# The last expert of a mixture-of-experts layer: where the other rows are normed and stored, and in what precision its down-projection runs

## The chip, the cores and the metric

The kernel runs on one core of a Trainium2 chip. The metric is the device time of one execution in microseconds (us), and the figure that counts is the median over runs. The engines are TensorE (PE, with its weight loads as PEld), VectorE (DVE), ScalarE (ACT), GpSimd (POOL) and SyncE (SP). Each runs its own instructions in order and waits for the others by semaphores. Transfers are issued from an engine's queue and carried out by 16 DMA engines that all queues share.

## The reference, cut to what matters

One layer works on 1024 latent tokens of 1024 features (float32). After a token mixer, the tokens `h` go through an expert-choice mixture of experts: each of 16 experts takes the 128 tokens with the highest affinity to it, and what the experts return is summed by token, normed, scaled and added to `h`.

```python
def ec_moe(x_tok, w_router, w_gate, w_up, w_down):
    t = x_tok.shape[1]
    cap = CAP_FACTOR * t // N_EXPERTS
...
    g, idx = lax.top_k(jnp.swapaxes(aff, 1, 2), cap)
    xs = jax.vmap(lambda xt, ix: xt[ix])(x_tok, idx)
    hg = jnp.einsum('becd,edf->becf', xs, w_gate)
    hu = jnp.einsum('becd,edf->becf', xs, w_up)
    y = jnp.einsum('becf,efd->becd', jax.nn.silu(hg) * hu, w_down) * g[..., None].astype(xs.dtype)
    return jax.vmap(lambda ix, val: jnp.zeros((t, D_MODEL), val.dtype)
                    .at[ix.reshape(-1)].add(val.reshape(-1, D_MODEL)))(idx, y)
...
        ff = ec_moe(xn, w_router[layer], w_gate[layer], w_up[layer], w_down[layer])
        h = h + g2 * rmsnorm(ff, norm_post_ffn[layer])
```

A token may be taken by several experts or by none, and its norm needs the sum over all of them. So no row that the last expert takes can be normed before that expert is done; the other rows can.

## The kernel before, in words

The part in question begins at line 1492 and fills the second half of the span. The 16 experts run one after the other. An expert's weights come as 24 tiles of 512 KB (six chunks of four: gate, up, gate, up, and two of the down-projection). `load_raw` (line 841) loads them on SP's queue into pages of two pools, 23 (`pgA`) and 7 (`pgX`), as early as pages come free; SP's order is the program's (`manual_schedule`). On the other engines the order is made by a scheduler at build time, from the program's order and its own estimates of durations.

`chunk` (line 1455) splits each tile on ScalarE and VectorE (`split`, line 161) into a high part `whi` and a rest `wlo`, both float32r. `mm3` (line 165) then makes one float32 product out of three float32r matmuls. The tokens `xh_`, `xl_` are split in the same way. `prod` (line 1467) makes `hg` and `hu`, 24 matmuls each for one half of the hidden features; `glu` (line 1486) makes `act` = silu(hg) * hu; `tsplit` (line 1448) transposes `act` on TensorE and splits it into `ach`, `acl`. The down-projection (line 1521) multiplies these by the last two chunks into two banks `pys`. For experts 0 to 14, `y` = `pys` times the gate value `g` is added to the rows `idx` of `ffS` in DRAM by an indirect scatter with accumulation, on POOL's queue (line 1534). `route(e + 1)` (line 1428) finds the next expert's rows and gathers them from `hS`, which holds `h`; `cur[2]` is the tile `xs` with the gathered rows. The output `out` has been filled with `h` long before.

The last expert's `y` does not go to DRAM. During its first `hg`, line 1509 makes `oht`, a one-hot matrix for each of the eight tiles of 128 tokens (`tt` holds the compared positions). At the end of the loop SP loads `bcG2` (the gain times the gate, broadcast) and the eight tiles of `ffS` into `fr` (line 1544). After the down-projection `y` is split into `yh`, `yl` (lines 1558 and 1559), and for each tile four matmuls with `oht` place the rows of `y` (`added`), two additions on VectorE put them onto `fr`, and a square on ScalarE sums each row (line 1582). Tiles are taken in pairs. `rsqrt` (line 215) is a chain of small VectorE steps, 13 for a pair and 10 for a single column. `final` (line 1562) scales `fr` by the root and by `bcG2` and adds it to `out` with an accumulating store on POOL's queue (line 1571).

Of the kernel before, what the change touches and what calls it, by code (L numbers as in the profile page):

```python
# [10 lines left out]
F32 = mybir.dt.float32  # L11
# [35 lines left out]
TGR = ((0, 1), (2, 3), (4, 5), (6, 7))  # L47
TD = 1
SUMB = ("ee", "eb", "bb", "ee", "be", "bb", "ee", "bb")
# [27 lines left out]
TA = (0, 2)  # L77
TP = ()
# [74 lines left out]
def build(tc, nc, I, out, dbg=None):  # L153
# [4 lines left out]
    def f(ap):  # L158
        return ap.bitcast(F32)

    def split(hi, lo, src, eng=V):
        S.activation(hi, src, AF.Copy)  # L162
        eng.tensor_sub(lo, src, f(hi))  # L163

# [6 lines left out]
    with es:  # L171
# [1282 lines left out]

        def chunk(e, c, eng=V):
            r = []
            for q in range(4):
                if not raws:
                    load_raw(pgX if (nraw[0] - NR0) % (NPA + NPX) < NPX else pgA)
                raw = raws.popleft()  # L1460
                hi = spl.tile([P, 2, 512], F32R, name="whi")
                lo = spl.tile([P, 2, 512], F32R, name="wlo")
                split(hi, lo, raw, eng)
                r.append((hi, lo))
            return r
# [20 lines left out]
        def glu(hg, hu):  # L1486
            a = x1.tile([P, 512], F32, name="act", bufs=2)
            S.activation(a, hg, AF.Silu)
            V.tensor_mul(a, a, hu)
            return a  # L1490

# [4 lines left out]
        for e in range(E):  # L1496
# [3 lines left out]
            for fh in range(2):  # L1500
                hg = eacc("hg")
                prod(hg, xh_, xl_, chunk(e, 2 * fh) if e or fh else first)
                if fh:
                    tsplit(acts[0], 0, ach, acl)
                elif e + 1 < E:
                    nxt = route(e + 1)
                else:

                    oht = page(pgA, "oht", F32R, (P, KT, P))
                    tt = sm.tile([P, KT], F32, name="tt")  # L1510
                    for t in range(KT):
                        V.tensor_scalar(tt[:, t:t + 1], cur[3][:, 0:1], -BIG - t * P, None, op0=OP.add)
                    V.tensor_tensor(out=oht, in0=late["iota"][:, None, :].to_broadcast([P, KT, P]),
                                    in1=tt[:, :, None].to_broadcast([P, KT, P]), op=OP.is_equal)
                hu = eacc("hu")
                prod(hu, xh_, xl_, chunk(e, 2 * fh + 1))
                acts.append(glu(hg, hu))
            if e + 1 < E:
                xh_, xl_ = xsplit(nxt[2], nxt[4])
            pys = [eacc("pyy") for _ in range(2)]  # L1520
            for c in range(2):
# [16 lines left out]
        fr = []  # L1538
        bc["G2"] = page(pgA, "bcG2")
        load_bc("G2")  # L1540
        for t in range(KT):

            fr.append(page(pgA, "ffr"))
            SY.dma_start(out=fr[t], in_=ffS[t * P:(t + 1) * P, :])
        yh, yl = page(pgA, "yh", F32R), page(pgA, "yl", F32R)
        fp = {}

        def sums(t):
            k = SUMB[t]
            return [bank([P, 512], "pff") if c == "b" else eacc("pff") for c in k]  # L1550

        def added(t):
            for dh, sl in enumerate(halves):
                PE.matmul(fp[t][dh], oht[:, t, :], yh[:, sl], start=True, stop=False)
                PE.matmul(fp[t][dh], oht[:, t, :], yl[:, sl], start=False, stop=True)

        for dh, sl in enumerate(halves):
            S.activation(yh[:, sl], pys[dh], AF.Copy, scale=g[:, 0:1])
            V.scalar_tensor_tensor(yl[:, sl], pys[dh], g[:, 0:1], f(yh[:, sl]), op0=OP.mult, op1=OP.subtract)
        sg, rg = [], []  # L1560

        def final(k):
            for j, t in enumerate(TGR[k]):
                r = rg[k][:, j:j + 1]
                if t in TA:
                    S.activation(fr[t], fr[t], AF.Copy, scale=r)
                elif t in TP:
                    V.tensor_scalar(fr[t], fr[t], r, None, op0=OP.mult)
                else:
                    V.scalar_tensor_tensor(fr[t], fr[t], r, bc["G2"], op0=OP.mult, op1=OP.mult)  # L1570
                G.dma_start(out=out[t * P:(t + 1) * P, :], in_=fr[t], accum_op=OP.add)

        for i, grp in enumerate(TGR):
            w = len(grp)
            ss = sm.tile([P, w], F32, name=f"ssf{w}")
            for k, t in enumerate(grp):
                junk = page(pgA, "sqf")
                fp[t] = sums(t)
                added(t)
                for dh, sl in enumerate(halves):  # L1580
                    V.tensor_add(fr[t][:, sl], fp[t][dh], fr[t][:, sl])
                S.activation(junk, fr[t], AF.Square, accum_out=ss[:, k:k + 1])
                if t in TA + TP:
                    G.tensor_mul(fr[t], fr[t], bc["G2"])
                if i and k == TD:
                    final(i - 1)
            rg.append(rsqrt(ss, D, w))
        final(len(TGR) - 1)
# [15 lines left out]
```

## Time and profile before

| | |
|---|---|
| time, median of 3 runs | 1399.57 us (1394.0 to 1402.64) |
| time of the profiled execution | 1401.37 us |
| its span | 1399.6 us |
| mean granted TensorE clock | 0.941 |
| TensorE busy | 1259.0 us (90%) |
| VectorE busy | 1104.3 us (79%) |
| ScalarE busy | 805.7 us (58%) |
| GpSimd busy | 70.8 us (5%) |
| moved to and from DRAM | 247 GB/s over the span |

Busy shares are means over stages with different limits, so they don't say what bounds a given stage. For that a stretch of the span is read by itself, in the views whose rows stand below. Matmuls are pipelined: the time from the start of one to the start of the next is what one costs. The profile was taken of one execution; its span is 1.8 us shorter than its time.

### The profile page before, as it was taken

The numbers are of one execution on the slowest core, as the hardware profiler recorded it, in microseconds if no ns is written. First come the engines' busy times: TensorE is split into PE (matmuls) and PEld (weight loads), VectorE is DVE, ScalarE is ACT, GpSimd is POOL, SyncE is SP. The second block draws the span as 40 slices with busy tenths as digits, with TensorE's granted clock in tenths as the row PEclk, the third lists the DMA queues.
The fourth block names the chain that finished last, engine by engine and source line by source line (L and its number), as shares of the span: only waits on it lengthen the run. The fifth ranks groups of instructions, "written<-read, shape, count | busy, mean of one in ns | idle before, by whom it ended". The sixth has DMA issues, their size and how long they took to land.

```text
span 1399.6 us, 18794 instructions
## 1 busy us (share of the span) xinstructions
PE 1259.0 (90%) x6457; PEld 1028.7 (73%) x6457; DVE 1104.3 (79%) x2005; ACT 805.7 (58%) x1191; POOL 70.8 (5%) x56
## 2 busy tenths in 40 slices
PE   6999998999989699789762999999999999999990
PEld 3587886887878578677652888888888888877770
DVE  6963666988778667698686799999999998888885
ACT  6632112443434444453331888888888888888762
POOL 0000000000000000000001000000000001201012
PEclk8999999999999899999775999999999999999995
DMA  9359456554486963432287899999999999999736
GB/s 351 117 109 325 133 159 208 162 164 136 142 160 182 235 218 110 136 124 95 76 311 275 278 364 389 374 376 376 379 373 378 377 379 379 354 345 350 267 120 120
DMA packets 143376, 346.67 MB, mean 248 GB/s; under 512 B 17456, under 2 KB 59952, under 8 KB 142640
## 3 DMA queue, kind: packets, MB, share of 16 engines
q1 hardware_dynamic: 115520, 310.34, 63.4%
q0 software_dynamic: 5616, 20.45, 6.1%
q10 hardware_dynamic: 22144, 14.68, 3.7%
q8 instruction: 51, 0.84, 0.2%
q14 instruction: 45, 0.37, 0.1%
HBM read 296.65 MB, written 48.77 MB: 247 GB/s over the span
## 4 chain that ended last, share of the span: by engine, by line
PE 47%; DVE 8%; ACT 2%; issue 1%; DMA 1%; SPq 0%; POOL 0%; POOLq 0%; ACTq 0%; DVEq 0%
PE hg L167 4%; PE hg L168 4%; PE hg L166 4%; PE hu L166 4%; PE hu L167 4%; PE hu L168 4%; PE pyy L167 4%; PE pyy L168 4%; PE pyy L166 4%; PE ptt L1479 2%; PE pl L921 1%; DVE nm L1099 1%; PE ptt L1451 1%; PE pf L799 1%; PE ps L1090 1%
## 5 line engine op out<-in xcount | busy, mean ns | idle before, releaser
L163 DVE TENSOR_TENSOR wlo<-raw,whi 128x1024 fp32r<-128x1024 f32 x384 | 450.1, 1221 | 30.8 <-ACT whi L162 24.5
L162 ACT ACTIVATE whi<-raw 128x1024 fp32r<-128x1024 f32 x384 | 396.1, 1066 | 61.7 <-PE hu L168 24.9
L1103 ACT ACTIVATE e<-ps,nm 128x1280 f32<-128x1280 f32 x64 | 84.4, 1325 | 68.5 <-DVE nm L1099 61.3
L1099 DVE TENSOR_REDUCE nm<-ps 128x1 f32<-128x1280 f32 x64 | 92.8, 1485 | 16.0 <-PE ps L1090 15.9
L167 PE MATMUL pyy<-wlo,ach 128*128 128x512 f32 x256 | 101.3, 396 | 3.5 <-DVE wlo L163 3.1
L166 PE MATMUL hu<-whi,xsh 128*128 128x512 f32 x256 | 101.9, 398 | 0.0
L168 PE MATMUL hg<-whi,xsl 128*128 128x512 f32 x256 | 101.2, 395 | 0.8 <-DVE xsl L163 0.8
L167 PE MATMUL hg<-wlo,xsh 128*128 128x512 f32 x256 | 101.8, 398 | 0.0
L166 PE MATMUL hg<-whi,xsh 128*128 128x512 f32 x256 | 101.3, 396 | 0.0
L167 PE MATMUL hu<-wlo,xsh 128*128 128x512 f32 x256 | 100.8, 394 | 0.0
L168 PE MATMUL pyy<-whi,acl 128*128 128x512 f32 x256 | 100.2, 391 | 0.0
L168 PE MATMUL hu<-whi,xsl 128*128 128x512 f32 x256 | 99.9, 390 | 0.0
L1135 ACT ACTIVATE ath<-ptr 128x512 fp32r<-128x512 f32 (+1 forms) x96 | 47.5, 525 | 90.7 <-PE ptr L1130 90.4
L166 PE MATMUL pyy<-whi,ach 128*128 128x512 f32 x256 | 98.9, 402 | 0.0
L1090 PE MATMUL ps<-KK,q 128*128 128x512 f32 (+1 forms) x384 | 91.0, 384 | 7.8 <-ACT e L1103 6.2
L1090 PEld LDWEIGHTS ps<-KK,q 128*128 128x128 f32 x384 | 65.1, 202 | 18.8 <-ACT e L1103 7.4
L679 PE MATMUL pf<-xh,wl 128*128 128x512 f32 x192 | 77.7, 405 | 0.0
L677 PE MATMUL pf<-xl,wh 128*128 128x512 f32 x192 | 77.3, 403 | 0.0
L675 PE MATMUL pf<-xh,wh 128*128 128x512 f32 x192 | 77.0, 401 | 0.0
L1138 DVE TENSOR_TENSOR atl<-ptr,ath 128x512 fp32r<-128x512 f32 (+1 forms) x96 | 55.6, 596 | 13.8 <-ACT ath L1135 13.6
L167 PEld LDWEIGHTS pyy<-wlo,ach 128*128 128x128 f32 x256 | 48.2, 188 | 18.0 <-DVE wlo L163 8.2
L167 PEld LDWEIGHTS hg<-wlo,xsh 128*128 128x128 f32 x256 | 48.9, 191 | 11.5 <-DVE wlo L163 1.1
(293 smaller groups left out, 2728.8 us busy)
## 6 DMA issues: line engine op xcount, KB each, us to landing
raw<-in_we SPq DMA_DIRECT2D x384, 512.0 KB, 9.5
wa<-in_wa SPq DMA_DIRECT2D x64, 256.0 KB, 4.8
wraw<-in_wF SPq DMA_DIRECT2D x20, 512.0 KB, 6.4
waw<-in_wa SPq DMA_DIRECT2D x16, 512.0 KB, 5.9
q<-qS SPq DMA_DIRECT2D x64, 128.0 KB, 4.9
mS<-hl SPq DMA_DIRECT2D x48, 128.0 KB, 4.2
vS<-hv ACTq DMA_DIRECT2D x20, 256.0 KB, 6.5
KK<-kS SPq DMA_DIRECT2D x16, 320.0 KB, 4.9
```

The source lines that it names most:

```text
L162: S.activation(hi, src, AF.Copy)
L163: eng.tensor_sub(lo, src, f(hi))
L166: PE.matmul(ps, wh, mh, start=first, stop=False)
L167: PE.matmul(ps, wh, ml, start=False, stop=False)
L168: PE.matmul(ps, wl, mh, start=False, stop=last)
L675: PE.matmul(ps, wh[:, kt, :], xh[kt][:, sl], start=first, stop=False)
L677: PE.matmul(ps, wh[:, kt, :], xl[kt][:, sl], start=False, stop=False)
L679: PE.matmul(ps, wl[:, kt, :], xh[kt][:, sl], start=False, stop=last)
L1090: PE.matmul(ps[:, m, k0:k0 + n], q[:, m, j, :], KK[:, m, k0:k0 + n], start=(j == 0), stop=(j == 1))
L1099: V.tensor_reduce(out=c[1][-1], in_=c[0][:, m, :], axis=AX.X, op=OP.max, negate=True)
L1103: S.activation(e, c[0][:, m, :], AF.Exp, bias=c[1][3 + m], accum_out=l[:, m:m + 1])
L1138: V.tensor_sub(x[1], x[2], f(x[0]))
```

## The change

- Before expert 15's first `hu`: `bcG2` is loaded (SP), the rows of `ffS` that the last expert takes are gathered into `ffg`, and the eight tiles of `ffS` are loaded into `fr`, both on POOL's queue. `oht` and `tt` are gone.
- `final(k)` now squares a pair of tiles of `fr` as they are after 15 experts, takes the root, scales and stores with accumulation onto `out`. Four calls stand between the steps of the last down-projection, at `i` = 0, 2, 4 and 6. `issue_after` puts the squares behind the last weight split and the last Silu on ScalarE. Rows that expert 15 takes get a value in `out` here that is overwritten later.
- The last down-projection uses the weight tiles as loaded, and `ach` as plain float32 (`tcopy` copies the transposed `act` without splitting it): 16 plain fp32 matmuls for 48 float32r ones, and no splits of the eight tiles.
- After it, the last expert's 128 rows are finished apart: `ffg` + `g` * `pys`, norm, gain, plus `cur[2]` (the same rows of `h`), and an indirect scatter onto `out` without accumulation. The `y` split, the one-hot matmuls, the additions and the constants of their order are gone.

```diff
--- before.py
+++ after.py
@@ -44,9 +44,6 @@
 NPT = 6
 NLZ = 3
 WOE = (1,) * 8
-TGR = ((0, 1), (2, 3), (4, 5), (6, 7))
-TD = 1
-SUMB = ("ee", "eb", "bb", "ee", "be", "bb", "ee", "bb")
 NL0 = 2
 NCF = 8
 NJK = 2
@@ -74,8 +71,6 @@
 SO = (2, 2)
 NMA = 2
 LAGX = 1
-TA = (0, 2)
-TP = ()
 IM = 0
 NEP = (0, 0, 0)
 NR0 = 10
@@ -159,8 +154,9 @@
         return ap.bitcast(F32)
 
     def split(hi, lo, src, eng=V):
-        S.activation(hi, src, AF.Copy)
+        i = S.activation(hi, src, AF.Copy)
         eng.tensor_sub(lo, src, f(hi))
+        return i
 
     def mm3(ps, wh, wl, mh, ml, first, last):
         PE.matmul(ps, wh, mh, start=first, stop=False)
@@ -1452,6 +1448,8 @@
             split(hi[:, k0:k0 + 4, :], lo[:, k0:k0 + 4, :], pp)
 
 
+        lasts = [None, None]
+
         def chunk(e, c, eng=V):
             r = []
             for q in range(4):
@@ -1460,7 +1458,7 @@
                 raw = raws.popleft()
                 hi = spl.tile([P, 2, 512], F32R, name="whi")
                 lo = spl.tile([P, 2, 512], F32R, name="wlo")
-                split(hi, lo, raw, eng)
+                lasts[0] = split(hi, lo, raw, eng)
                 r.append((hi, lo))
             return r
 
@@ -1485,9 +1483,30 @@
 
         def glu(hg, hu):
             a = x1.tile([P, 512], F32, name="act", bufs=2)
-            S.activation(a, hg, AF.Silu)
+            lasts[1] = S.activation(a, hg, AF.Silu)
             V.tensor_mul(a, a, hu)
             return a
+
+        fr = []
+
+        def tcopy(src, k0, to):
+            pp = bank([P, 4, P], "ptt")
+            for j in range(4):
+                PE.transpose(out=pp[:, j, :], in_=src[:, j * P:(j + 1) * P], identity=ident)
+            S.activation(f(to[:, k0:k0 + 4, :]), pp, AF.Copy)
+
+        def final(k):
+
+            ss = sm.tile([P, 2], F32, name="ssf")
+
+            with tc.issue_after(lasts[0].ins), tc.issue_after(lasts[1].ins):
+                for j in range(2):
+                    S.activation(page(pgA, "sqf"), fr[2 * k + j], AF.Square, accum_out=ss[:, j:j + 1])
+            r = rsqrt(ss, D, 2)
+            for j in range(2):
+                t = 2 * k + j
+                V.scalar_tensor_tensor(fr[t], fr[t], r[:, j:j + 1], bc["G2"], op0=OP.mult, op1=OP.mult)
+                G.dma_start(out=out[t * P:(t + 1) * P, :], in_=fr[t], accum_op=OP.add)
 
         first = chunk(0, 0)
         cur = route(0)
@@ -1500,24 +1519,41 @@
             for fh in range(2):
                 hg = eacc("hg")
                 prod(hg, xh_, xl_, chunk(e, 2 * fh) if e or fh else first)
-                if fh:
+                if fh and e + 1 == E:
+                    tcopy(acts[0], 0, ach)
+                elif fh:
                     tsplit(acts[0], 0, ach, acl)
                 elif e + 1 < E:
                     nxt = route(e + 1)
                 else:
-
-                    oht = page(pgA, "oht", F32R, (P, KT, P))
-                    tt = sm.tile([P, KT], F32, name="tt")
+                    bc["G2"] = page(pgA, "bcG2")
+                    load_bc("G2")
+
+                    ffg = page(pgA, "ffg")
+                    G.indirect_dma_start(out=ffg, out_offset=None, in_=ffS[:, :],
+                                         in_offset=bass.IndirectOffsetOnAxis(ap=idx[:, :1], axis=0))
                     for t in range(KT):
-                        V.tensor_scalar(tt[:, t:t + 1], cur[3][:, 0:1], -BIG - t * P, None, op0=OP.add)
-                    V.tensor_tensor(out=oht, in0=late["iota"][:, None, :].to_broadcast([P, KT, P]),
-                                    in1=tt[:, :, None].to_broadcast([P, KT, P]), op=OP.is_equal)
+                        fr.append(page(pgA, "ffr"))
+                        G.dma_start(out=fr[t], in_=ffS[t * P:(t + 1) * P, :])
                 hu = eacc("hu")
                 prod(hu, xh_, xl_, chunk(e, 2 * fh + 1))
                 acts.append(glu(hg, hu))
             if e + 1 < E:
                 xh_, xl_ = xsplit(nxt[2], nxt[4])
             pys = [eacc("pyy") for _ in range(2)]
+            if e + 1 == E:
+
+                for i in range(KT):
+                    if i == TSJ:
+                        tcopy(acts[1], 4, ach)
+                    if i % 2 == 0:
+                        final(i // 2)
+                    if not raws:
+                        load_raw(pgX if (nraw[0] - NR0) % (NPA + NPX) < NPX else pgA)
+                    raw = raws.popleft()
+                    for dh in range(2):
+                        PE.matmul(pys[dh], f(ach[:, i, :]), raw[:, dh, :], start=i == 0, stop=i == KT - 1)
+                continue
             for c in range(2):
                 w = chunk(e, 4 + c)
                 for j in range(4):
@@ -1535,57 +1571,16 @@
                                      in_=y, in_offset=None, compute_op=OP.add)
                 cur = nxt
 
-        fr = []
-        bc["G2"] = page(pgA, "bcG2")
-        load_bc("G2")
-        for t in range(KT):
-
-            fr.append(page(pgA, "ffr"))
-            SY.dma_start(out=fr[t], in_=ffS[t * P:(t + 1) * P, :])
-        yh, yl = page(pgA, "yh", F32R), page(pgA, "yl", F32R)
-        fp = {}
-
-        def sums(t):
-            k = SUMB[t]
-            return [bank([P, 512], "pff") if c == "b" else eacc("pff") for c in k]
-
-        def added(t):
-            for dh, sl in enumerate(halves):
-                PE.matmul(fp[t][dh], oht[:, t, :], yh[:, sl], start=True, stop=False)
-                PE.matmul(fp[t][dh], oht[:, t, :], yl[:, sl], start=False, stop=True)
-
+        sl2 = sm.tile([P, 2], F32, name="ssl")
         for dh, sl in enumerate(halves):
-            S.activation(yh[:, sl], pys[dh], AF.Copy, scale=g[:, 0:1])
-            V.scalar_tensor_tensor(yl[:, sl], pys[dh], g[:, 0:1], f(yh[:, sl]), op0=OP.mult, op1=OP.subtract)
-        sg, rg = [], []
-
-        def final(k):
-            for j, t in enumerate(TGR[k]):
-                r = rg[k][:, j:j + 1]
-                if t in TA:
-                    S.activation(fr[t], fr[t], AF.Copy, scale=r)
-                elif t in TP:
-                    V.tensor_scalar(fr[t], fr[t], r, None, op0=OP.mult)
-                else:
-                    V.scalar_tensor_tensor(fr[t], fr[t], r, bc["G2"], op0=OP.mult, op1=OP.mult)
-                G.dma_start(out=out[t * P:(t + 1) * P, :], in_=fr[t], accum_op=OP.add)
-
-        for i, grp in enumerate(TGR):
-            w = len(grp)
-            ss = sm.tile([P, w], F32, name=f"ssf{w}")
-            for k, t in enumerate(grp):
-                junk = page(pgA, "sqf")
-                fp[t] = sums(t)
-                added(t)
-                for dh, sl in enumerate(halves):
-                    V.tensor_add(fr[t][:, sl], fp[t][dh], fr[t][:, sl])
-                S.activation(junk, fr[t], AF.Square, accum_out=ss[:, k:k + 1])
-                if t in TA + TP:
-                    G.tensor_mul(fr[t], fr[t], bc["G2"])
-                if i and k == TD:
-                    final(i - 1)
-            rg.append(rsqrt(ss, D, w))
-        final(len(TGR) - 1)
+            V.scalar_tensor_tensor(ffg[:, sl], pys[dh], g[:, 0:1], ffg[:, sl], op0=OP.mult, op1=OP.add)
+            S.activation(page(pgA, "sqf")[:, sl], ffg[:, sl], AF.Square, accum_out=sl2[:, dh:dh + 1])
+        V.tensor_add(sl2[:, 0:1], sl2[:, 0:1], sl2[:, 1:2])
+        r = rsqrt(sl2[:, 0:1], D, 1)
+        V.scalar_tensor_tensor(ffg, ffg, r[:, 0:1], bc["G2"], op0=OP.mult, op1=OP.mult)
+        V.tensor_add(ffg, ffg, cur[2])
+        G.indirect_dma_start(out=out[:, :], out_offset=bass.IndirectOffsetOnAxis(ap=idx[:, :1], axis=0),
+                             in_=ffg, in_offset=None)
         e6.close()
         e4.close()
         eM.close()
```

## Rows read from the trace of the kernel before

**Rows 1.** Busy time by stretch: us, each engine's busy time, granted clock, DMA share, GB/s

```profile
core 0: us, PE busy (x) PEld busy (x) DVE busy (x) ACT busy (x) POOL busy (x), PEclk, DMA share, GB/s
1320.00:1345.00 25.00, 25.00 (x108) 19.27 (x107) 21.63 (x20) 19.39 (x22) 1.91 (x1) 1.00 0.76 264
...
1356.00:1374.00 18.00, 10.12 (x35) 6.22 (x33) 17.21 (x50) 10.36 (x17) 5.95 (x4) 0.79 0.00 1
1374.00:1396.00 22.00, 0.00 (x0) 0.00 (x0) 8.46 (x27) 2.19 (x3) 5.87 (x7) 0.50 1.02 190
```

**Rows 2.** One line's instructions, L1571: issue in ns, first and last start, landing

```profile
L1571 POOL DMA_DIRECT2D out_y<-ffr x8: 862/864/1263, 1372.8 to 1383.0; - x8
...
DMA to landing us min/median/max: 5.5/10.5/14.2
```

**Rows 3.** Timeline of TensorE, last down-projection: start us, us, engine, line, operation, operands

```profile
1344.87 0.62 PE L166 MATMUL pyy<-whi,ach 128*128 128x512 f32 x2
...
1346.23 0.60 PE L1451 MATMUL ptt<-ident,act 128*128 128x128 f32 x4
...
1356.07 0.39 PE L168 MATMUL pyy<-whi,acl 128*128 128x512 f32 x1
```

**Rows 4.** One line's instructions, L1544: SP's loads of `ffS`

```profile
L1544 SPq DMA_DIRECT2D ffr<-ffS x8: 327/389/522, 1329.1 to 1332.5; - x8
...
DMA to landing us min/median/max: 3.6/4.4/9.9
```

**Rows 5.** Timeline of TensorE: plain fp32 matmuls, in expert 9 and near the start

```profile
1120.09 1.95 PE L1479 MATMUL ptt<-dgx,xs 128*128 128x128 f32 x16
1121.79 0.48 PE L166 MATMUL pyy<-whi,ach 128*128 128x512 f32 x1
...
13.90 5.29 PE L363 MATMUL pm<-waw,silu 128*2 128x512 f32 x8 [3.60 <-DMA waw<-in_wa]
```

**Rows 6.** POOL's gathers (L1439) and scatter-adds (L1534) by line, and its timeline

```profile
L1439 POOL DMA_INDIRECT xs<-hS,idx x16: 997/1627/4937, 758.3 to 1280.0; - x16
...
DMA to landing us min/median/max: 4.4/8.2/12.0
...
L1534 POOL DMA_INDIRECT ffS<-y,idx x15: 1591/1595/2713, 809.3 to 1322.5; - x15
...
DMA to landing us min/median/max: 6.6/10.1/11.1
...
1322.49 1.91 POOL L1534 DMA_INDIRECT ffS<-y,idx  x1 [35.55 <-ACT y L1533]
```

**Rows 7.** SP's waits from 1240 us, and the last 15 tile loads (L845) by line

```profile
SPq L845 <- DVE wlo L163: 38.6, 24, 12.3
...
L845 SPq DMA_DIRECT2D raw<-in_we x15: 327/430/2378, 1300.0 to 1315.1; - x15
...
DMA to landing us min/median/max: 4.4/9.6/10.9
```

**Rows 8.** Timeline of ScalarE from expert 15 to the end

```profile
1339.83 4.91 ACT L162 ACTIVATE whi<-raw 128x1024 fp32r<-128x1024 f32 x5
1346.87 0.60 ACT L162 ACTIVATE ach<-ptt 128x512 fp32r<-128x512 f32 x1 [2.12 <-PE ptt L1451]
...
1359.49 1.06 ACT L1582 ACTIVATE sqf<-ffr 128x1024 f32<-128x1024 f32 x1 [2.18 <-DVE ffr L1581]
...
1360.68 1.06 ACT L1582 ACTIVATE sqf<-ffr 128x1024 f32<-128x1024 f32 x1
```

**Rows 9.** Timeline of VectorE; its first line is the group of weight subtractions from 1344 us

```profile
L163 DVE TENSOR_TENSOR wlo<-raw,whi 128x1024 fp32r<-128x1024 f32 x8 | 9.3, 1222 | 0.0
...
1345.07 0.69 DVE L1489 TENSOR_TENSOR act<-act,hu 128x512 f32<-128x512 f32 x1 [0.65 <-PE hu L168]
...
1356.77 1.41 DVE L1559 SCALAR_TENSOR_TENSOR yl<-pyy,slot,yh 128x512 fp32r<-128x512 f32 x2 [2.46 <-ACT yh L1558]
...
1379.02 0.15 DVE L208 TENSOR_TENSOR nz<-nz 128x2 f32<-128x2 f32 x1
...
1380.19 2.48 DVE L1570 SCALAR_TENSOR_TENSOR ffr<-ffr,nz,bcG 128x1024 f32<-128x1024 f32 x2
```

## The prediction, made before the changed kernel was run

> **What bounds the kernel now.** I read the table of stretches first [rows 1]. From 1320 to 1345 us TensorE is busy in every microsecond at a granted clock of 1.00: the last of the 16 experts is bound by matmuls. Then the engines hand the bound on. From 1356 to 1374 VectorE is busy 17.2 of 18.0 us, TensorE only 10.1, and the DMA engines move nothing. From 1374 to 1396 the DMA engines are full (share 1.02, 190 GB/s) and the others mostly idle. The last down-projection matmul starts at 1356.07 [rows 3], so 43 us of the span follow it: first a stretch of VectorE, then one of stores. The view of the stores [rows 2] shows the second: eight accumulating stores of 512 KB, the first issued at 1372.8, the last at 1383.0 and landing 14.2 us later, at 1397.2; the span ends 2.4 us after that. From first issue to last landing the train takes 24.4 us. The eight loads of `ffS` do not bound: they start at 1329.1, when expert 14's scatter-add has landed, and take 3.6 to 9.9 us each [rows 4], under matmuls.
>
> The reader should see that the 24.4 us of DMA train have nothing in front of them but a chain that begins after the last expert. The change is worth as much as it issues the first store earlier, less what it puts behind the last one.
>
> **The change, part by part.**
>
> *Removed behind the down-projection.* The split of the last `y`, 32 one-hot matmuls, 16 additions and all the work of the norms: everything between 1356.1 and 1372.8. Also the `oht` comparison and eight `tt` additions on VectorE during the last two experts; TensorE is the full engine there, so I take zero for them (a gain of at most one pass over 1024 columns, 1.2 us [rows 9], and eight tiny steps if VectorE set the pace).
>
> *Down-projection in plain fp32.* Before, 48 matmuls and four transposes took from 1344.87 to 1356.5, 11.6 us [rows 3]. Now 16 plain fp32 matmuls of 512 columns. Line 1479 is plain fp32 already: eight source matmuls of 128 columns appear as 16 records, 1.70 us from the first start to the next instruction [rows 5], so 0.21 us each, 0.85 us for 512 columns, 13.6 us for 16. The other bound is line 363, 512 columns near the start of the span: eight records in 5.29 us are 1.32 us a source matmul, 21.2 us for 16; that engine had just waited for loads. I take 13.6, from the row of the same stage. With four transposes (0.6 us) TensorE ends at 1344.9 + 14.2 = 1359.1, 2.6 us later than before. Eight splits on ScalarE and eight subtractions on VectorE go: both are free after the fourth chunk of expert 15.
>
> *Loads of `ffS` on POOL's queue.* They and the new gather `ffg` stand behind expert 14's scatter-add (issued 1322.49 [rows 6]) and wait until it lands at 1329.1, as SP did. With 1.6 us for issuing the gather and 0.86 us a load [rows 2, 6], fr1 is issued at 1331.6 and lands, at 4.4 us (median load) to 12.0 us (slowest gather), between 1336.0 and 1343.6; the eighth is issued by 1337.6. Behind them POOL has only the stores. SP loses eight issues and takes `G2`'s load ahead of the last 20 weight tiles instead of behind them: one more transfer among them, hidden by their lead, as follows.
>
> *Ten pages held.* `bcG2`, `ffg` and eight `ffr` now take ten of 30 pages ahead of the last 20 weight tiles. SP waits for pages already [rows 7], so tiles come later by the use of ten tiles. Fifteen scatters from 809.3 to 1322.5 [rows 6] make an expert 36.7 us and a tile 1.53, so 15.3 us. The last tile was issued at 1315.1 [rows 7] and is used in the last products before 1356: some 35 us of lead. That leaves about 20, against at most 10.9 to land. I cost it at zero; it costs when the lead falls below 10.9.
>
> *Squares and first store.* `issue_after` holds the squares behind the last weight split and the second Silu. Of the five splits in the row from 1339.83 [rows 8], the first two are the last of the fourth chunk, so ScalarE is free at 1341.8. Two squares with their reads, 1.2 us from start to start: 1344.2. The inverse root is 13 small dependent VectorE steps, 0.195 us each where nothing else runs (six of them from 1379.02 to 1380.19 [rows 9]): 2.5 us. The `act` product of 0.7 comes between: 1347.4. One scale, 1.24: **the first store is issued at 1348.6** instead of 1372.8. What VectorE owes by then for all four pairs (eight scales, 9.9, and 52 steps, at most 10.1) is done by 1365, so a store comes at least every 2.3 us, faster than the train takes them (24.4 / 8 = 3.1).
>
> *Store train.* 24.4 us as before: 1373.0. Bounds: the full stretch alone is 22.0 us [rows 1]; loads still in flight when it starts could add some 2.5.
>
> *The last expert's own rows.* TensorE ends at 1359.1; scale and add 0.7, square at most 1.2, one addition 0.2, a root of ten steps 2.0, passes of 1.24 and 1.22 [rows 8, 9]: 1365.7, or 1371.6 if it all queues behind VectorE's last norm. The scatter writes rows that the stores add to, so it waits for the last landing, 1373.0. A scatter that only writes is not in the trace. Bounds from issue to landing: 3.6 us (fastest load [rows 4]) and 10.1 us (median scatter-add, beside weight traffic [rows 6]). I take 4.4, the fastest gather of the same size and form, since the DMA is empty then: 1377.4. With the 2.4 us of ending: **1379.8**.
>
> The Trainium skill, DMA: Bandwidth & Descriptors, section Anatomy of one DMA, gives a transfer from GpSimd's queue about 2 us plus its bytes at 436 GB/s. For 512 KB that is an estimate of 3.2 us, with which the sum would be 1378.6. No run here shows it; the fastest gather took 4.4.
>
> The span goes from 1399.6 to 1379.8, 19.8 us less. The profiled execution took 1401.4 us, 0.1% above the median of 1399.57; I subtract from the median.
>
> **The rivals.**
>
> *Squares behind the copy.* If ScalarE's order puts the copy of the transposed `act` (ending 1347.5 [rows 8]) before the first square, the train starts 5.7 us later: 1385.5. For it: that order is fixed ahead, by estimates of when loads land. Against: the squares stand first in the program. If they fall behind the whole down-projection, so that the change does not do what it says, the train starts 17 us later: 1397.
>
> *POOL is held up by VectorE.* The gather and two loads would each wait out one weight subtraction of 1.22 us, or three of them: 4 to 11 us, so 1384 to 1391. Against: the scatter issued at 1322.49 beside such subtractions took 1.91 us, the median is 1.60 [rows 6]. The Trainium skill, SBUF — State Buffer, in its summary of rules, wants a DMA that is to hide under VectorE work issued from SP or ACT, because GpSimd can be locked out while it writes descriptors; by that rule this change moves nine issues the wrong way. The trace bears out 0.3 us an issue.
>
> *The last rows decide.* TensorE would have to end over 7.3 us later. At the lower clock (0.50 from 1374 on, when TensorE has run dry [rows 1]) the 13.6 us become 27.2, and the end 1386. Against: it has no gap in which to fall.
>
> *No wait behind the stores.* If the scatter queues without waiting for the last landing, some 4.4 us go: 1375.5.
>
> *Slower than before.* All eight squares stand ahead of the `act` copy on ScalarE, and TensorE waits for fr7. From its landing L: square and copy 1.9, eight matmuls at the lower clock 13.6, the last rows 6.6, scatter and end 6.8, so L + 28.9. This passes 1399.6 from L = 1370.7, that is, if the 4.7 MB after 1331 move at under 119 GB/s. Stores on POOL's queue moved 190 alone; at half of that, sharing with weights, L is 1380.7 and the end 1410. For it: the tail of the weights now shares the DMA. Against: before, the last of these loads landed by 1342.4 (1332.5 and 9.9 us [rows 4]).
>
> **How the numbers follow.** Forecast 0.58; squares behind the copy 0.14, behind everything 0.05; POOL held 0.07; last rows 0.05; no wait 0.07; slower 0.04. The forecast's own range comes from its bounds: 1375.9 (train 22.0, scatter 3.6, no `act` between) to 1388.6 (fr1 0.6 late, shared train, scatter 10.1), most of it in 1376 to 1386. The range for eight in ten, 1374 to 1389, leaves out the squares behind everything, the slow case, half of POOL held and the tails. One per cent, about what a measurement of this kernel can tell from no change, is 14 us, so faster means under 1385.6: the forecast, the early case and about half of the copy, POOL and last-row cases, 0.77. Slower by more than that is half of the slow case, 0.02. The rest, 0.21, is within 1%.
>
> **What would show it.** Right: the first store issued near 1348.6, the DMA full until about 1372 at some 200 GB/s, the scatter issued when the last store lands with VectorE long done, and TensorE without a gap from 1345 to 1359 in 32 records of the fp32 product. Wrong: TensorE waiting in the down-projection, fr0 landing after 1342, a slower train beside other traffic, or a last scatter of much over 5 us.

## The result, and the profile after

Median 1380.85 us (four runs, 1379.99 to 1386.75), against 1399.33 for the kernel before (four runs): ratio 0.987, 95% interval 0.983 to 0.991, so faster by 1.3% (the interval ends at 0.9%). The profiled execution took 1380.93 us, its span 1379.2. Predicted: 1380.0, in 1374 to 1389, faster by more than 1%. But in that agreement an error of the forecast met the luck of one execution, and to see both the span must be cut.

The POOL timeline of the changed kernel (start, us, line, out<-in; in brackets the idle time before and what ended it):

```profile
1316.58 1.58 POOL L1570 DMA_INDIRECT ffS<-y,idx  x1 [35.56 <-DMA raw<-in_we]
1327.15 1.31 POOL L1533 DMA_INDIRECT ffg<-ffS,idx  x1 [8.99 <-DMA raw<-in_we]
...
1348.78 0.89 POOL L1509 DMA_DIRECT2D out_y<-ffr  x1 [12.31 <-DVE ffr L1508]
...
1361.38 0.85 POOL L1509 DMA_DIRECT2D out_y<-ffr  x1 [0.35 <-DVE ffr L1508]
1372.95 1.03 POOL L1582 DMA_INDIRECT out_y<-ffg,idx  x1 [10.72 <-DMA out_y<-ffr]
```

The first store goes out at 1348.78 (1372.8 before [rows 2]); the last scatter waits 10.72 us for the stores, is issued at 1372.95, and the span ends 6.2 us later. But expert 14's scatter, the last thing that both kernels do alike, is issued at 1316.58 and not at 1322.49 [rows 6]: 5.9 us early. Up to there TensorE, ScalarE and GpSimd execute the same instructions in the same order; VectorE lacks only the nine that made `tt` and `oht`, and SP's queue differs from `bcG2`'s load on (1275.04). Those differences come too late to explain it: expert 0's scatter, 515 us earlier, where the two programs are still alike, is already 7.7 us early. First the kernel before, then the changed one:

```profile
809.31 1.61 POOL L1534 DMA_INDIRECT ffS<-y,idx  x1 [38.64 <-ACT y L1533]
```

```profile
801.63 1.60 POOL L1570 DMA_INDIRECT ffS<-y,idx  x1 [35.83 <-ACT y L1569]
```

Measured from expert 14's scatter to the end of the span, the kernel before takes 77.1 us and this profile 62.6: 14.5 less, where 57.3, that is 19.8 less, was forecast.

Where the missing 5.3 us went stands in the timeline of ScalarE, first of the kernel before, then of the changed one:

```profile
1322.11 3.89 ACT L162 ACTIVATE whi<-raw 128x1024 fp32r<-128x1024 f32 x4
1327.31 0.60 ACT L1488 ACTIVATE act<-hg 128x512 f32<-128x512 f32 x1 [1.32 <-PE hg L168]
1327.81 4.89 ACT L162 ACTIVATE whi<-raw 128x1024 fp32r<-128x1024 f32 x5
```

```profile
1316.20 2.00 ACT L157 ACTIVATE whi<-raw 128x1024 fp32r<-128x1024 f32 x2
1321.38 0.60 ACT L1486 ACTIVATE act<-hg 128x512 f32<-128x512 f32 x1 [3.19 <-PE hg L164]
1321.88 3.88 ACT L157 ACTIVATE whi<-raw 128x1024 fp32r<-128x1024 f32 x4
...
1341.42 1.05 ACT L1504 ACTIVATE sqf<-ffr 128x1024 f32<-128x1024 f32 x1
```

Before, four tiles of the next product are split ahead of the Silu of expert 15's first `hg`; now two. ScalarE stands 3.19 us in front of the Silu, and only then splits the two tiles that `hu` needs. TensorE's waits, and its granted clock in four stretches (duration, then busy us and instructions of PE, PEld, DVE, ACT, POOL, then the granted clock, the DMA share and GB/s):

```profile
PE hu L162 <- ACT whi L157: 1.6, 1, 1.6
PE hu L163 <- DVE wlo L158: 0.8, 1, 0.8
```

```profile
1314.50:1321.00 6.50, 6.46 (x29) 4.99 (x27) 3.77 (x4) 3.27 (x4) 1.58 (x1) 1.00 1.00 345
1321.00:1324.50 3.50, 1.11 (x4) 0.45 (x3) 1.54 (x2) 3.12 (x4) 0.00 (x0) 0.86 1.06 305
1324.50:1330.20 5.70, 5.70 (x14) 4.44 (x15) 4.31 (x4) 3.19 (x4) 3.04 (x5) 0.50 1.02 389
1330.50:1340.00 9.50, 9.50 (x44) 7.37 (x43) 6.45 (x6) 5.48 (x7) 2.31 (x5) 1.00 1.03 421
```

A wait of 2.4 us, and after it 5.7 us in which TensorE works without a pause at a granted clock of 0.50, the 1.2 GHz level, with matmuls 0.43 us apart instead of 0.23: some 3 us more. That is 5.4.

Why ScalarE's order changed: SP, which loads the tiles in the program's order, now meets the ten new pages. Its timeline, and its waits from 1270 to 1350:

```profile
1275.04 0.33 SPq L905 DMA_DIRECT2D bcG<-bS  x1
1299.79 44.16 SPq L841 DMA_DIRECT2D raw<-in_we  x20
```

```profile
SPq L841 <- DVE wlo L158: 42.8, 13, 24.3
SPq L841 <- ACT sqf L1504: 15.2, 2, 14.6
```

SP stands 24.3 us for a page and issues the last 20 tiles from 1299.8 to 1343.6, where before the last went out at 1315.1 [rows 7]. They still land in time: the four splits behind the Silu run without a wait, and the last tile lands some 8 us before its first matmul. But the delay is larger than the working had it: the last tile is issued 27.0 us after the scatter, where before it was issued 7.4 us ahead of it, so 34 us later and not 15.3. In the second line of the waits SP stands 14.6 us for a square on ScalarE: the squares write their unused output to scratch pages `sqf`, which come from the same pool and are not among the ten.

None of that makes the gap by itself. But the scheduler, which fixed ScalarE's order at build time from its own estimates, put the Silu ahead of two splits of such late tiles. That the late pages are the cause is shown below, where the loads alone are moved and the old order returns.

### The profile page after: what moved, and what is told of

Its sections match the earlier page's. It is cut to its first block, busy times and chain, and to the rows that moved or that the text cites. A ratio compares the mean times of both kernels' runs of the same rounds, so it can differ in the third digit from the quotient of the medians.

```text
span 1379.2 us, 18653 instructions
## 1 busy us (share of the span) xinstructions
PE 1248.1 (90%) x6409; PEld 1016.5 (74%) x6409; DVE 1088.7 (79%) x1985; ACT 795.4 (58%) x1183; POOL 68.3 (5%) x64
## 5 line engine op out<-in xcount | busy, mean ns | idle before, releaser
L158 DVE TENSOR_TENSOR wlo<-raw,whi 128x1024 fp32r<-128x1024 f32 x376 | 440.9, 1220 | 33.9 <-ACT whi L157 28.7
L157 ACT ACTIVATE whi<-raw 128x1024 fp32r<-128x1024 f32 x376 | 388.7, 1067 | 63.9 <-PE hu L164 28.3
L1095 DVE TENSOR_REDUCE nm<-ps 128x1 f32<-128x1280 f32 x64 | 92.7, 1483 | 21.1 <-PE ps L1086 21.0
L163 PE MATMUL pyy<-wlo,ach 128*128 128x512 f32 x240 | 95.7, 399 | 3.5 <-DVE wlo L158 3.2
L164 PE MATMUL pyy<-whi,acl 128*128 128x512 f32 x240 | 94.5, 394 | 0.0
L162 PE MATMUL pyy<-whi,ach 128*128 128x512 f32 x240 | 94.3, 405 | 0.0
L163 PEld LDWEIGHTS pyy<-wlo,ach 128*128 128x128 f32 x240 | 45.4, 189 | 17.1 <-DVE wlo L158 7.7
L162 PEld LDWEIGHTS hu<-whi,xsh 128*128 128x128 f32 x256 | 48.8, 191 | 11.7 <-ACT whi L157 2.1
```

The costliest lines, as they stand in the source:

```text
L157: i = S.activation(hi, src, AF.Copy)
L162: PE.matmul(ps, wh, mh, start=first, stop=False)
L163: PE.matmul(ps, wh, ml, start=False, stop=False)
L164: PE.matmul(ps, wl, mh, start=False, stop=last)
L1095: V.tensor_reduce(out=c[1][-1], in_=c[0][:, m, :], axis=AX.X, op=OP.max, negate=True)
```

## The experiments

One table first, since all are read in the same way: times from expert 14's scatter, in each kernel's profile, and the median, with its ratio to the kernel before run beside it.

| kernel | first store | last scatter issued | end | median us, ratio to before (95%) |
|---|---|---|---|---|
| before | 50.3 | none | 77.1 | 1399.33 |
| changed | 32.2 | 56.4 | 62.6 | 1380.85, 0.987 (0.983 to 0.991) |
| after_again | 30.7 | 56.7 | 62.9 | 1384.96, 0.989 (0.986 to 0.992) |
| after_third | 29.4 | 53.5 | 59.6 | 1381.40, 0.987 (0.984 to 0.990) |
| e4_fp32only | 53.1 | none | 79.0 | 1405.42, 1.004 (1.002 to 1.007) |
| e3_split | 34.2 | 62.4 | 68.6 | 1393.36, 0.994 (0.992 to 0.997) |
| e1_pages | 41.5 | 66.9 | 73.1 | 1394.89, 0.996 (0.995 to 0.998) |
| e2_silu | 29.8 | 54.9 | 61.1 | 1381.94, 0.988 (0.984 to 0.992) |
| e5_plain | 29.3 | 48.7 | 54.9 | 1375.93, 0.984 (0.981 to 0.987) |
| e9_vorder | 31.6 | 56.7 | 62.9 | 1384.05, 0.989 (0.986 to 0.992) |
| e8_order | 28.0 | 53.4 | 59.5 | 1383.40, 0.989 (0.987 to 0.991) |
| e10_chain | 28.0 | 53.9 | 60.1 | 1378.38, 0.984 (0.981 to 0.987) |
| e10_again | 28.0 | 53.8 | 60.0 | 1383.39, 0.988 (0.985 to 0.990) |

**The changed kernel again, twice** (`after_again`, `after_third`). The same kernel, nothing edited.

> The changed kernel once more, beside the next three. Theory (its profile's earlier stages were 5.9 us ahead of the kernel before by the luck of that one execution, and its last expert loses 5.3 us to a TensorE gap): from the issue of expert 14's scatter to the span's end 62 to 63.5 us again, the gap at expert 15's first hu product there again, wherever the scatter falls in time; median 1379 to 1383. Rival (the change itself makes the earlier stages faster): the scatter is issued near 1316.6 again, about 6 us ahead of the kernel before.

> The changed kernel a third time, beside the next one on the same chip. From expert 14's scatter to the span's end 62.5 to 63 us, as in its two profiles; median 1381 to 1385.

The scatter was issued at 1320.31 and 1319.17, so the 5.9 us were luck and no gain of the change. Expert 0's scatter falls between 801.3 and 810.8 in the profiles of this study (809.31 before; 801.63, 805.43 and 804.27 in the three of the changed kernel), and from there to expert 14's it is 513 to 515 us in all of them. The second end, 62.9, agreed, but its median, 1384.96, missed its 1379 to 1383; the third end, 59.6, missed its 62.5, with its median inside. TensorE's wait was the same 1.6 and 0.8 us in all three. What differs is the clock behind it, here the second profile's, then the third's:

```profile
1325.00:1328.20 3.20, 0.81 (x3) 0.42 (x3) 1.52 (x2) 3.09 (x4) 0.00 (x0) 0.90 1.06 291
1328.50:1330.90 2.40, 2.40 (x7) 1.88 (x6) 2.40 (x3) 1.39 (x3) 0.05 (x1) 0.50 1.02 386
```

```profile
1323.50:1327.00 3.50, 1.11 (x5) 0.37 (x4) 1.43 (x2) 3.00 (x4) 0.00 (x0) 1.00 1.06 301
1327.00:1333.00 6.00, 6.00 (x27) 4.93 (x28) 4.92 (x5) 4.51 (x5) 3.43 (x5) 1.00 1.02 395
```

After the same wait TensorE worked at the lower level for 5.7 us, 2.4 us, and not at all. So the gap costs 2.4 us for certain and up to 3 more by the clock, and behind the scatter the change is worth 14.2 to 17.5 us against the one profile of before.

**One part alone: plain fp32 in the kernel before** (`e4_fp32only`).

```diff
-            for c in range(2):
+            for i in range(KT if e + 1 == E else 0):
...
+                    PE.matmul(pys[dh], f(ach[:, i, :]), raw[:, dh, :], start=i == 0, stop=i == KT - 1)
```

> The kernel before with one part of the change alone: the last down-projection in plain fp32, everything behind it as before. Theory: TensorE ends 2.6 us later, nothing is gained behind it, 1402 (0.2% slower). Rival (the eight splits and subtractions held the down-projection up): 1396 to 1399.

1.9 us more behind the scatter, about what the step on it said (2.6 for TensorE), and slower by 0.4%: alone it costs. The median, 1405.42, is 3.4 us over the 1402 expected. The profile is of one of the two fastest of ten executions, and where the others lose more is not shown.

**The other part alone: the down-projection split again** (`e3_split`).

```diff
...
-                        PE.matmul(pys[dh], f(ach[:, i, :]), raw[:, dh, :], start=i == 0, stop=i == KT - 1)
+                        mm3(pys[dh], ach[:, i, :], acl[:, i, :], hi[:, dh, :], lo[:, dh, :], i == 0, i == KT - 1)
```

> The changed kernel with its last down-projection as before: eight more weight splits on ScalarE, eight subtractions on VectorE, three float32r matmuls a product. Squares stand between the splits. Theory (the store train decides, and plain fp32 is worth what it takes off ScalarE and VectorE): TensorE would end 2.6 us earlier but for its waits, VectorE gets 10.5 us more to do and becomes the last engine, the last stores are issued after 1366, and the time is 1383 to 1387. Rival (TensorE's end decides): 1378 to 1379.

6 us more than the changed kernel's own first profile, 9 more than the third, which like this one kept the high clock after the gap at `hu`; the median missed its 1383 to 1387, being 6 us over it. Waits of TensorE, and VectorE's timeline:

```profile
PE pyy L163 <- DVE wlo L158: 5.5, 3, 4.7
```

```profile
1360.83 2.48 DVE L1508 SCALAR_TENSOR_TENSOR ffr<-ffr,nz,bcG 128x1024 f32<-128x1024 f32 x2
1363.30 1.22 DVE L158 TENSOR_TENSOR wlo<-raw,whi 128x1024 fp32r<-128x1024 f32 x1
1364.51 1.22 DVE L158 TENSOR_TENSOR wlo<-raw,whi 128x1024 fp32r<-128x1024 f32 x1
1365.91 1.23 DVE L158 TENSOR_TENSOR wlo<-raw,whi 128x1024 fp32r<-128x1024 f32 x1
1367.05 2.48 DVE L1508 SCALAR_TENSOR_TENSOR ffr<-ffr,nz,bcG 128x1024 f32<-128x1024 f32 x2
...
1372.20 0.75 DVE L1574 SCALAR_TENSOR_TENSOR ffg<-pyy,slot,ffg 128x512 f32<-128x512 f32 x1 [0.67 <-PE pyy L164]
```

Subtractions and norms take turns on VectorE: TensorE waits 5.5 us for the one, the stores for the other, and the last store goes out 54.1 us after the scatter (44.8 in the changed kernel). Two things add to it. After its wait TensorE works at the lower clock again (granted 0.50 from 1364.6 to 1370.3), and in the last line the last rows' first product stands ahead of the last norm and waits for TensorE. How the 6 to 9 us divide among the three is not shown. Still the parts need each other: plain fp32 costs 1.9 us alone and is worth 6 to 9 beside the norms, where it takes eight subtractions off the engine that they need.

**All tiles ahead of the new pages** (`e1_pages`).

```diff
+                    while nraw[0] < 24 * E:
+                        load_raw(pgX if (nraw[0] - NR0) % (NPA + NPX) < NPX else pgA)
                     bc["G2"] = page(pgA, "bcG2")
```

> The changed kernel with one difference: all weight tiles of expert 15 get their pages ahead of bcG2, ffg and the eight ffr, as in the kernel before. Theory: in the changed kernel the ten pages, taken early, push the last 20 weight loads back in the scheduler's reckoning, and it therefore queues the first Silu of expert 15 ahead of two weight splits on ScalarE; TensorE loses 2.0 + 0.8 us of waiting and some 3 us at the lower clock. With the pages late SP's wait of 24 us for a page goes, Silu stands behind four splits again, and TensorE has no gap between 1315 and 1345. In this build, however, all eight squares stand behind the copy of the transposed act, so of these 5.5 us the first store gains only 1 or less: 1379 to 1381. Rival (the gap comes from somewhere else, for example weights that land late because the DMA is shared): the gap stays and the time is 1384 to 1387, since the squares are then late as well.

Both times missed: 1394.89. But TensorE's gap was gone and ScalarE's order was that of before, which shows that the displaced loads cause the gap. ScalarE's timeline, with four splits ahead of the Silu:

```profile
1323.84 3.89 ACT L157 ACTIVATE whi<-raw 128x1024 fp32r<-128x1024 f32 x4
1329.04 0.60 ACT L1486 ACTIVATE act<-hg 128x512 f32<-128x512 f32 x1 [1.30 <-PE hg L164]
...
1349.12 0.60 ACT L1496 ACTIVATE ach<-ptt 128x512 f32<-128x512 f32 x1 [5.52 <-PE ptt L1495]
```

The scheduler moved something else. VectorE's and POOL's timelines:

```profile
1360.29 1.61 DVE L1578 SCALAR_TENSOR_TENSOR ffg<-pyy,slot,ffg 128x512 f32<-128x512 f32 x2 [11.91 <-PE pyy L1557]
1364.17 2.48 DVE L1508 SCALAR_TENSOR_TENSOR ffr<-ffr,nz,bcG 128x1024 f32<-128x1024 f32 x2
```

```profile
1365.76 0.89 POOL L1509 DMA_DIRECT2D out_y<-ffr  x1 [28.49 <-DVE ffr L1508]
```

On VectorE the last rows' first product stood ahead of all norms and waited 11.9 us for TensorE; on ScalarE all eight squares stood behind the second copy into `ach` (1349.12), the rival of the prediction.

**Only the Silu moved** (`e2_silu`).

```diff
...
+                with tc.issue_after(spls[-3].ins):
+                    lasts[1] = S.activation(a, hg, AF.Silu)
```

> The changed kernel with one difference: the first Silu of expert 15 is put behind the same two weight splits as before, pages left as in the changed kernel. Theory (the order on ScalarE costs the gap, the tiles themselves had landed by 1314): the gap of TensorE at 1321 goes, the last hu ends 5 us earlier against the start of the expert; the first square then waits for fr0, which lands some 10 us after its issue under the shared DMA, so the first store gains 3 to 5 us: 1376 to 1378. Rival (tiles land late, so the order does not matter): ScalarE waits for the tiles, no gain, 1381.

The gap was gone and ScalarE was free 19.4 us after the scatter (24.8 in the changed kernel's first profile, 19.3 forecast), but the end came only 1.5 us earlier than in that profile, inside the 59.6 to 62.9 of the three. The median, 1381.94, missed its 1376 to 1378; it is near the rival's figure, but the rival's mechanism, tiles that land late, is not what is seen, since the gap went. Waits of ScalarE:

```profile
ACT sqf L1510 <- DMA ffr<-ffS: 5.2, 6, 1.3
```

The squares now wait for their loads, which take 14.9 us in the median, beside the tiles that SP was late with; with all tiles ahead (`e8_order`) the same loads take 7.2. So the displaced tiles cost a second time: as traffic.

**Tiles ahead, and VectorE's order set (`e9_vorder`); then ScalarE's too (`e8_order`).** The first moves the tile loads as above and holds the last rows' product behind the last norm:

```diff
...
+            with tc.issue_after(lasts[2].ins):
+                V.scalar_tensor_tensor(ffg[:, sl], pys[dh], g[:, 0:1], ffg[:, sl], op0=OP.mult, op1=OP.add)
```

> The kernel with all tile loads issued ahead of the new pages, and on VectorE the last rows' first product held behind the last norm. Theory (the loss of the first of these experiments comes from that product standing ahead of the norms on VectorE, where it waited 11.9 us for TensorE): squares start some 25.4 us after expert 14's scatter as there, the first store follows 7 to 8 us later, so some 33 us after the scatter against 41.5 there and 32.2 in the changed kernel; the end 62 to 64 us after it; time 1380 to 1384, some 10 to 12 us less than that experiment. Rival (the squares' place behind the copy of ach is the whole loss): 1392 to 1396 as there.

First store at 31.6, end at 62.9 and not 73.1: of the 10.5 us that the tiles-ahead kernel lost to the changed one's first profile, 10.2 were VectorE's order; the median, 1384.05, is at the edge of its range. The second also puts four squares ahead of the copy and each pair's norm behind the one before:

```diff
...
+                        with tc.issue_after(lasts[3].ins):
+                            tcopy(acts[1], 4, ach)
...
```

> As the one before, and also on ScalarE the first four squares ahead of the second copy into ach, and on VectorE each pair's norm behind the pair before. Theory (with tiles ahead and both orders set, ScalarE is free some 19 us after expert 14's scatter): the first store 25 to 27 us after the scatter, the train 23.4 us, the end 56 to 58 us after the scatter against 62.6 in the changed kernel; time 1374 to 1376.5, some 5 to 6 us less than the changed kernel. Rival (TensorE now waits for the copy behind four squares, and the last rows come after the train): the end 58 to 61 us after the scatter, time 1377 to 1380.

Its timeline on ScalarE and on POOL:

```profile
1337.74 1.05 ACT L1504 ACTIVATE sqf<-ffr 128x1024 f32<-128x1024 f32 x1
```

```profile
1318.46 1.58 POOL L1579 DMA_INDIRECT ffS<-y,idx  x1 [35.51 <-ACT y L1578]
...
1346.46 0.89 POOL L1513 DMA_DIRECT2D out_y<-ffr  x1 [14.99 <-DVE ffr L1512]
...
1361.94 0.85 POOL L1513 DMA_DIRECT2D out_y<-ffr  x1 [0.35 <-DVE ffr L1512]
1371.81 1.03 POOL L1592 DMA_INDIRECT out_y<-ffg,idx  x1 [9.02 <-DMA out_y<-ffr]
```

ScalarE is free at 19.3 us, as forecast. The first store comes at 28.0, not at 25 to 27: in VectorE's order the root's steps stand behind the `act` product, which waits for `hu`. The end at 59.5 misses 56 to 58, and the median, 1383.40, misses both ranges; the train took 25.4 us. The end is inside the rival's 58 to 61, but not by its mechanism: TensorE has no wait in the down-projection, and the last scatter waits for the stores.

**One chain of small steps for six tiles** (`e10_chain`, `e10_again`).

```diff
...
+                        squares(4, 8)
+                        final(2, 6)
...
```

> As the kernel with all tiles ahead and both orders set, but the first two tiles are normed alone and the other six with one chain of small steps over six columns. Theory (there VectorE's four chains, 4.76 us a pair, delivered the last store 15.5 us after the first; the accumulating stores themselves need some 20 us for 4 MB at 205 to 210 GB/s and a start and an end around it): first store 28 us after expert 14's scatter as there, last store issued some 39 instead of 43.5 us after it, the final scatter issued 51.5 instead of 53.4 us after it, the end 57.5 us after it against 59.5 there and 62.6 and 62.9 in the two profiles of the changed kernel; time 1377 to 1382 by where the scatter falls. Rival (the stores' transfers set the whole train, VectorE's pace none of it): the end 59 to 60 us after the scatter as there, time 1380 to 1384.

> The kernel with tiles ahead, both orders and one chain for six tiles, a second time. Theory (its last expert is 2.5 us shorter than the changed kernel's, 60.1 against 62.6 and 62.9 in the profiles, and the rest of its lower median was where the earlier stages fell): the end 59.5 to 60.5 us after the scatter, median 2 to 3 us under the changed kernel's of the same call, ratios to the kernel before within each other's intervals. Rival (it is 4 us or more faster, as its first median said): the end near 58 us after the scatter, median 4 to 6 us lower.

The last store and the last scatter on POOL (expert 14's scatter is at 1324.38):

```profile
1364.09 0.85 POOL L1516 DMA_DIRECT2D out_y<-ffr  x1 [0.35 <-DVE ffr L1515]
1378.26 1.03 POOL L1598 DMA_INDIRECT out_y<-ffg,idx  x1 [13.33 <-DMA out_y<-ffr]
```

The last store went out 39.7 us after the scatter instead of 43.5, and the end came at 60.1 and 60.0, not at 57.5: the pace at which VectorE delivers the last stores is not what sets the train. The low first median did not come back: the second, 1383.39, is 2.0 us over the changed kernel's beside it (1381.40), where 2 to 3 under were expected. By the runs, none of these versions is shown to beat the changed kernel.

**Stores that only write** (`e5_plain`).

```diff
-                G.dma_start(out=out[t * P:(t + 1) * P, :], in_=fr[t], accum_op=OP.add)
+                G.dma_start(out=out[t * P:(t + 1) * P, :], in_=fr[t])
```

> The changed kernel with its eight stores writing instead of accumulating; what is left out is the addition of h to the rows that the last expert does not take. Theory (the train of accumulating stores sets the end, at some 210 GB/s): the stores land as they come, the last near 1364 to 1366 on the changed kernel's clock, the last rows (ready 5.0 us before the train's end there) decide, and the time is 4 to 5 us less, 1376 to 1377. Rival (the train is set by the pace at which VectorE and ScalarE deliver, not by the accumulation): no change, 1380 to 1382.

1375.93, a little under the theory's figure. DMA issues of the changed kernel, then of this one (KB each, median us to landing), and this one's last row on POOL:

```profile
out_y<-ffr POOLq DMA_DIRECT2D x8, 512.0 KB, 8.6
```

```profile
out_y<-ffr POOLq DMA_DIRECT2D x8, 512.0 KB, 3.0
```

```profile
1366.94 1.00 POOL L1582 DMA_INDIRECT out_y<-ffg,idx  x1 [6.27 <-DVE ffg L1581]
```

A store lands in 3.0 us where an accumulating one takes 8.6, and now the last rows end the wait. Against the third profile of the changed kernel, whose first store stands at the same place, the end is 4.7 us earlier. That is the least that the accumulation costs, since the last rows now decide: the last store has landed 45.0 us after the scatter, some 8 us ahead of the last accumulating one there.

## Why the prediction was right, and where it was wrong

Its mechanism held: the train of stores moved under the last expert, and the end follows the train. Step by step, from the scatter on, with the first profile of the changed kernel:

- *Ten pages held, at zero.* This step failed. The working asked only whether late tiles land before their use. They do, though the delay was mis-sized, 34 us for 15.3: 14.6 us of it is the wait for a square's scratch page, which the working left out. The cost came by ScalarE's order, which the change of SP's order rearranged: 2.4 us of wait, up to 3 by the clock. The same tiles then slowed the scatter ahead of the loads of `ffS` (9.8 us to landing, 6.6 before) and the loads (11.7 in the median; with all tiles ahead, in `e8_order`, the gather behind the scatter goes out after 6.9 and the loads take 7.2), so that fr1 lands 22.7 us after the scatter's issue, past the latest bound, 21.1; hidden here, since ScalarE was later still.
- *Squares and first store.* ScalarE free at 24.8 instead of 19.3, all of it from the gap; the first store at 32.2 instead of 26.1. Without the gap (`e8_order`) 19.3 and 28.0: the rest, 1.9, is the root queued behind the `act` product, which itself waits for `hu` until 23.5 us after the scatter (22.6 before [rows 9]): the working added the product's 0.7 us and not that wait.
- *Store train.* 24.2 us from the first issue to the last scatter's, 24.4 forecast; 24.1 to 26.0 in the other profiles whose stores follow at once. The DMA is full while it runs, at 193 to 215 GB/s in each 2 us from 1352 to 1370 (two of these rows):

```profile
1358.00:1360.00 2.00, 1.02 (x3) 0.19 (x1) 1.88 (x5) 0.00 (x0) 0.07 (x1) 1.00 1.07 193
1368.00:1370.00 2.00, 0.00 (x0) 0.00 (x0) 0.00 (x0) 0.00 (x0) 0.00 (x0) 0.50 1.07 211
```

- *Plain fp32.* No gap from 1346.8 on; 28 of the 32 records in 12.18 us, 0.87 us a matmul (0.85 forecast); the other four were pulled ahead between `hu`'s. TensorE ends 42.4 us after the scatter, where 36.6 was forecast, and in `e8_order`, without the gap, 36.9:

```profile
1346.83 12.18 PE L1555 MATMUL pyy<-raw,ach 128*128 128x512 f32 x28
```

- *The last rows.* VectorE takes them up at 1361.0, right behind its last norm, and is done at 1367.9. That is 51.3 us after the scatter, past the bounds of 43.2 to 49.1 that the working gives from there, but still 5 us before the scatter's turn:

```profile
1361.00 1.40 DVE L1576 SCALAR_TENSOR_TENSOR ffg<-pyy,slot,ffg 128x512 f32<-128x512 f32 x2
...
1366.68 1.22 DVE L1581 TENSOR_TENSOR ffg<-ffg,xs 128x1024 f32<-128x1024 f32 x1
```

- *Scatter and ending.* 3.4 and 2.8 us, 4.4 and 2.4 forecast. The Trainium skill's estimate (DMA: Bandwidth & Descriptors, Anatomy of one DMA) of 3.2 was nearer.
- *POOL held up by VectorE.* Not seen: the eight loads took 0.53 to 0.61 us of POOL each and the gather 1.31, beside weight subtractions. The Trainium skill (SBUF — State Buffer, summary of rules) states its rule for VectorE in a 2x or 4x mode, a condition that the prediction left out. Whether a subtraction here ran in one, no run shows.

The sum: +6.1 to the first store, -0.2 train, -0.6 scatter and ending, so 62.6 instead of 57.3. That the profiled 1380.93 is yet so near to 1380.0 is luck: in that execution the stages before were 5.9 us earlier by themselves. The forecast should be held against all sixteen executions of the changed kernel, in three groups with medians of 1380.85, 1384.96 and 1381.40: the median of all is 1382.3, 2 us over the forecast.

## What to carry to other kernels

When an edit takes buffers from a stage, count every buffer that it takes, scratch included, and do not ask only whether the data still lands in time: where a scheduler fixes the order of the in-order engines, later loads also rearrange what other engines do first, and a busy engine's 2 us gap can be paid twice, through its clock. Two edits that share an engine must be costed together, not one by one. And compare profiles from a common event (here a scatter), not from the start: the 800 us ahead of expert 0's scatter vary by 9.5 us between these profiles, more than most of the differences that are to be explained.

## What the runs showed of the hardware

The same wait of 2.4 us on TensorE was followed by 5.7, 2.4 or 0 us of work at the lower clock level in three executions of one program, and by none in two more kernels with the same wait (`e3_split`, `e5_plain`). An accumulating store of 512 KB, eight in a row, moved at 193 to 215 GB/s and landed after 8.6 us in the median; a writing one after 3.0. Issuing it took POOL 0.85 and 0.53 us.
